# Adaptive-modulation sums in a two-layer trunk: the vector engine's multiply-add replaced by an activation-engine multiply and an accumulating DMA

## The chip, the cores and the metric

The kernel runs on one core of one Trainium2 chip. The metric is the device time of one execution in microseconds (us), as the median of several runs. The profile is one more execution of the same program, recorded instruction by instruction.

## The reference

Two layers of a trunk with 512 tokens of width 1024, all in float32. Each layer has two sub-layers (a token mixer, then a squared-ReLU MLP with 4096 hidden units); layer 0 mixes with chunked attention (16 heads of 64), layer 1 with a gated spatial MLP. Around every sub-layer stands a modulation that depends on the vector `c` alone:

```python
cond = jax.nn.silu(c)
for i in range(DEPTH):                                  # DEPTH = 2
    mod = cond @ ada_w[i] + ada_b[i]                    # (1, 1024) @ (1024, 6144)
    sh1, sc1, g1, sh2, sc2, g2 = jnp.split(mod, 6, axis=-1)
    h = rms_norm(x, norm_mix[i]) * (1.0 + sc1) + sh1
    y = mixer(h)                                        # attention, then gMLP
    x = x + g1 * y
    h = rms_norm(x, norm_ffn[i]) * (1.0 + sc2) + sh2
    x = x + g2 * squared_relu_mlp(h, ffn_w1[i], ffn_w2[i])
```

The change concerns `cond @ ada_w[i]`, a product of one row with a matrix. There are 12 such products of 1024 by 1024, called (layer, m) with m = 0 to 5 for `sh1, sc1, g1, sh2, sc2, g2`.

## The kernel before, in words

**Matrix products.** Nearly all time goes to TensorE. Each float32 operand is split into a high part (a cast on ACT) and a low part (a subtraction on DVE), and each product is three matmuls (`mm3`; line 92 is the one call to the matmul). Weights come by DMAs that SP issues; lines 388/389 (`wload`), 405/406 (`wload_slabs`) and 483/484 (`Split`) are the casts and subtractions.

**Buffers.** All large tiles are 4 KB per partition and come from 49 slots in a ring (`Slots`): `get` takes the slot longest free, `free` puts it at the end. A DMA into a slot waits until the last reader of its former content is done, and SP issues its DMAs in order, so one late release holds up all loads behind it.

**Order.** The program's text gives priorities, and a planner with a simulated timeline fixes, before the run, the order of the instructions on every engine. Stretches between `in_order` and `any_order` keep the text's order on the engines named (always on PE). `tc.issue_after(x)` keeps the instructions of its block, on x's engine alone, behind x. On the chip each engine then works off its own list in that order and stops at any instruction whose inputs are late.

**Modulation.** The first two vectors, (0, 0) and (0, 1), are made by special code in the opening 70 us (line 948) and are not touched. The other ten go through a background queue `bgq`, in the order (0,2), (0,4), (0,3), (0,5), (1,1), (1,0), (1,2), (1,4), (1,3), (1,5). Each of them is nine items: eight parts and one end.

- A part loads 128 partitions x 1024 columns of `ada_w` (512 KB, line 179, issued by SP) into a slot `raw`. Row p, part k holds weight row 8p + k. `use` multiplies it by `cs[:, k]`, one number for each partition, and adds it to `acc`: line 192 for part 0 (a multiply into `acc`), line 194 for parts 1 to 7. Then `done()` frees `raw`.
- The end adds up the 128 partitions of `acc`. For m = 0, 1, 3, 4 (`ada_columns`): eight transposes on PE (line 207), reductions on DVE (208), the bias and the gain. For m = 2, 5 (`ada_rows`): a cast on ACT (232), a subtraction on DVE (233), matmuls with a matrix of ones through line 92, and the bias added on DVE (240).

`bg(n)` takes n items off the queue at chosen places of the text: 27 items during attention (2 after the key projection, 5 around the first head, then 2 a head for eight heads and 1 a head for four), 27 in the first MLP and the first part of layer 1, three at a time in the MLP, and the rest in the gate, in the `u` blocks and in the second MLP. In attention an item is loaded as it is taken; from the first MLP on, `lead[0] = 2` loads two items ahead. The uses run inside `behind()`, which is `tc.issue_after(mark[0].ins)`; `mark` is always a DVE instruction.

**Attention.** For each head, `head_a` loads a bias tile and POOL (GpSimd) clears a corner of it (line 1168); for each second head it makes keys and queries (lines 1139 to 1153, with SBUF to SBUF copies that SP issues at 1153). `head_b` multiplies scores on PE, then takes bias and row maxima on DVE (1190) and the exponential on ACT (1195); POOL widens the reciprocals for each pair (1200). `head_c` transposes (1228) and splits (1232, 1233); `head_d` multiplies by the values and applies POOL's widened rows (1263, 1265). `filler` puts the remaining projections between the heads. Apart from a few fills at the start, POOL has no other work than lines 1168, 1200 and two fills at 1475.

Of the kernel before, what the change touches and what calls it, by code (L numbers as in the profile page):

```python
# [12 lines left out]
AF = mybir.ActivationFunctionType  # L13
ALU = mybir.AluOpType
# [38 lines left out]
def trunk_kernel(  # L53
# [20 lines left out]
    V, A, G, T, SP = nc.vector, nc.scalar, nc.gpsimd, nc.tensor, nc.sync  # L74
# [80 lines left out]
    def raw_tile(shape):  # L155

        t, i = SL.get(shape, F32)
        return t, lambda: SL.free(i)

    def flat(src, offset, ap):  # L160
        return bass.AP(tensor=src.tensor, offset=src.offset + offset, ap=ap)
# [6 lines left out]
    def ada_acc(l, ms, c0, n, box):  # L168


        nm = len(ms)
        kl = D // n // nm

        def load(k0):
            box[k0] = raw, done = raw_tile([P, kl, nm * n])
            if nm == 1:
                w, base = (4096, D * 2048 - 2048) if l == 0 else (6144, D * 6144)
                src = flat(ada_w, base + k0 * w + ms[0] * D, [[KD * w, P], [1, D]])
                SP.dma_start(raw[:, 0, :], src)
            else:  # L180
                src = flat(ada_w, (c0 // n * P * KD + k0) * 512, [[KD * 512, P], [1, kl * 512]])
                SP.dma_start(raw.rearrange("p k n -> p (k n)"), src)

        def use(k0):
            if k0 == 0:
                box["acc"], box["id"] = SL.get([P, nm * n], F32)
            acc = box["acc"]
            raw, done = box.pop(k0)
            for k in range(k0, k0 + kl):
                r, ck = raw[:, k - k0, :], cs[:, k:k + 1]  # L190
                if k == 0:
                    V.tensor_scalar(acc, r, ck, None, ALU.mult)
                else:
                    V.scalar_tensor_tensor(acc, r, ck, acc, ALU.mult, ALU.add)  # L194
            done()

        return [(lambda k=k: load(k), lambda k=k: use(k)) for k in range(0, KD, kl)]
# [324 lines left out]
    class Spent:  # L522
# [33 lines left out]
        def done(self, m):  # L556
            self.op.pop(m).free()
# [1080 lines left out]
```

## Time and profile before

| | |
|---|---|
| median of 3 runs | 1421.3 us (1420.83 to 1423.51) |
| the profiled execution | 1422.04 us |
| its span in the trace | 1420.1 us |
| matmuls on PE | 1390.1 us busy, 98% of the span |
| DVE / ACT / POOL | 1021.5 / 712.1 / 9.1 us busy |
| moved by DMAs | 208.94 MB |

How to read it: PE, DVE, ACT, POOL and SP are TensorE, VectorE, ScalarE, GpSimd and SyncE; PEld is the loading of TensorE's weights. L194 is line 194 of the kernel. "A <- B" in a group of instructions means that A writes and B is read (s a slot, p a PSUM bank); in a view of waits it means that A waited for B. A "q" behind an engine's name is its instruction queue, so SPq is SP issuing DMAs. "The chain that ended last" is followed back from the last instruction, at each step to what released it. PE's busy time comes from modelled ends, so a busy PE may still lose some of its pace; its granted clock (PEclk, 1.00 is full) stands in the views by stretches.

### The profile page before, as it was taken

What the parts mean: (1) busy time and instruction counts of PE and PEld (TensorE: products, weight loads), DVE (VectorE), ACT (ScalarE), POOL (GpSimd) and SP (SyncE); (2) the same over time, 40 slices, a digit from 0 to 9 for tenths busy, and PEclk for the clock granted to TensorE, in tenths of its full rate; (3) what the DMA queues carried; (4) which work ended last, traced back from release to release, by engine and by line L of the source; (5) the groups of instructions that cost most, each with busy time, mean ns of one, the idle gap of its engine ahead of it and who ended that gap; (6) DMA issues with size and microseconds to landing.
All of it is one profiled execution on the core that took longest, in us unless ns stands there. A gap on an engine that the chain in (4) does not pass through costs nothing.

```text
span 1420.1 us, 18904 instructions
## 1 busy us (share of the span) xinstructions
PE 1390.1 (98%) x7222; PEld 1191.5 (84%) x7222; DVE 1021.5 (72%) x1494; ACT 712.1 (50%) x1230; POOL 9.1 (1%) x34
## 2 busy tenths in 40 slices
PE   9999989899999999999999999999999999999998
PEld 8888888779888888888888887888889988888887
DVE  6888889585676887786895745657577376766883
ACT  6546658555464544447577343134346355454630
POOL 0000000000000000000000000000000000000000
PEclk8999999999999999999999999999999999999999
DMA  9656465574245361357133344335337225142041
GB/s 373 236 152 205 141 190 150 181 258 157 63 152 186 119 212 55 111 190 263 60 104 119 119 133 134 97 127 185 119 119 280 77 75 192 53 156 89 30 163 60
DMA packets 82171, 208.94 MB, mean 147 GB/s; under 512 B 7576, under 2 KB 8992, under 8 KB 82080
## 3 DMA queue, kind: packets, MB, share of 16 engines
q1 hardware_dynamic: 82080, 207.72, 44.6%
q8 instruction: 57, 0.93, 0.3%
q14 instruction: 34, 0.28, 0.1%
HBM read 190.92 MB, written 8.39 MB: 140 GB/s over the span
## 4 chain that ended last, share of the span: by engine, by line
PE 86%; DMA 6%; DVE 5%; ACT 1%; issue 1%; SPq 0%; DVEq 0%; ACTq 0%
PE p L92 84%; DMA s<-in_ada_w 2%; DMA s<-in_a_w_in 2%; DMA s<-in_ffn_w 1%; DMA s<-s 1%; PE p L1536 1%; DVE s L194 1%; DVE s L389 1%; DVE s L1190 1%; PE p L315 1%; DMA s<-in_b_w_in 0%; DMA s<-in_a_w_out 0%; PE p L1228 0%; DVE s L1144 0%; DVE s L948 0%
## 5 line engine op out<-in xcount | busy, mean ns | idle before, releaser
L92 PE MATMUL p<-s,s 128*128 128x512 f32 (+3 forms) x6568 | 1327.6, 362 | 11.5 <-DVE s L1233 4.3
L92 PEld LDWEIGHTS p<-s,s 128*128 128x128 f32 x6568 | 1114.3, 190 | 198.0 <-DVE s L1233 4.9
L484 DVE TENSOR_TENSOR s<-s,s 128x1024 fp32r<-128x1024 f32 x234 | 280.6, 1221 | 112.1 <-PE p L92 53.8
L483 ACT CAST s<-s 128x1024 fp32r<-128x1024 f32 x234 | 241.6, 1051 | 176.3 <-PE p L92 111.3
L389 DVE TENSOR_TENSOR s<-s,s 128x1024 fp32r<-128x1024 f32 x80 | 96.6, 1221 | 60.8 <-ACT s L388 54.2
L388 ACT CAST s<-s 128x1024 fp32r<-128x1024 f32 x80 | 83.7, 1052 | 81.7 <-DMA s<-in_b_w_in 28.1
L631 DVE TENSOR_TENSOR s<-s,s 128x1024 f32<-128x1024 f32 x64 | 77.4, 1221 | 37.0 <-DMA s<-in_ffn_w 33.9
L194 DVE SCALAR_TENSOR_TENSOR s<-s,cs,s 128x1024 f32<-128x1024 f32 x70 | 89.7, 1281 | 12.3 <-DMA s<-in_ada_w 11.4
L739 ACT ACTIVATE r<-p 128x512 f32<-128x512 f32 x64 | 38.1, 595 | 115.2 <-PE p L92 115.2
L517 DVE TENSOR_TENSOR s<-p,s 128x512 f32<-128x512 f32 x104 | 70.6, 687 | 34.5 <-PE p L92 33.3
L745 ACT ACTIVATE s<-r 128x256 f32<-128x256 f32 (+1 forms) x112 | 44.9, 443 | 1.2
L424 DVE TENSOR_TENSOR tr<-p,s 128x512 f32<-128x512 f32 (+1 forms) x33 | 22.0, 672 | 30.3 <-PE p L92 30.1
L1195 ACT ACTIVATE s<-s,nm 128x128 f32<-128x128 f32 (+3 forms) x64 | 35.7, 560 | 6.3 <-DVE nm L1190 6.2
L1517 ACT CAST s<-s 128x512 fp32r<-128x512 f32 x24 | 14.5, 620 | 44.1 <-DVE s L1515 25.6
L1228 PE MATMUL p<-ident,s 128*128 128x128 f32 x160 | 25.3, 277 | 11.1 <-DVE s L1265 2.7
L1542 DVE TENSOR_TENSOR s<-p,s 128x256 fp32r<-128x256 f32 x48 | 20.0, 419 | 21.7 <-ACT s L1541 21.7
L1513 ACT ACTIVATE s<-p 128x512 f32<-128x512 f32 x24 | 14.4, 598 | 39.9 <-PE p L92 39.7
L530 DVE TENSOR_TENSOR s<-s,s 128x1024 f32<-128x1024 f32 x28 | 33.6, 1220 | 1.0 <-PE p L92 0.9
L304 ACT ACTIVATE s<-s 128x512 f32<-128x512 f32 x24 | 15.3, 636 | 35.5 <-DVE s L425 35.5
L1190 DVE CUSTOM_DVE_ANT_0 s<-p,s 128x128 f32<-128x128 f32 (+3 forms) x64 | 29.1, 486 | 4.6 <-PE p L92 2.7
L1228 PEld LDWEIGHTS p<-ident,s 128*128 128x128 f32 x160 | 18.4, 141 | 14.7 <-ACT s L1305 3.0
L1233 DVE TENSOR_TENSOR s<-p,s 128x512 fp32r<-128x512 f32 (+3 forms) x64 | 28.9, 484 | 2.4 <-ACT s L1232 2.2
(142 smaller groups left out, 766.5 us busy)
## 6 DMA issues: line engine op xcount, KB each, us to landing
s<-in_ffn_w SPq DMA_DIRECT2D x128, 512.0 KB, 4.6
s<-in_ada_w SPq DMA_DIRECT2D x96, 512.0 KB, 4.7
s<-in_b_w_in SPq DMA_DIRECT2D x48, 512.0 KB, 4.7
s<-in_b_w_out SPq DMA_DIRECT2D x24, 512.0 KB, 4.6
s<-in_a_w_in SPq DMA_DIRECT2D x22, 512.0 KB, 5.0
s<-s SPq DMA_DIRECT2D x64, 128.0 KB, 2.6
s<-in_x SPq DMA_DIRECT2D x8, 512.0 KB, 5.0
s<-in_a_rel_bias SPq DMA_DIRECT2D x16, 256.0 KB, 2.9
```

What stands on the lines that cost most here:

```text
L92: T.matmul(ps, lhsT, rhs, start=start, stop=stop, skip_group_check=more)
L194: V.scalar_tensor_tensor(acc, r, ck, acc, ALU.mult, ALU.add)
L388: A.copy(hi, raw)
L389: engs[len(ids) // 2 % len(engs)].tensor_tensor(lo, raw, f32(hi), ALU.subtract)
L483: A.copy(self.hi, raw)
L484: mark[0] = V.tensor_tensor(self.lo, raw, f32(self.hi), ALU.subtract)
L517: V.tensor_tensor(dst, ps, dst, ALU.add)
L631: V.tensor_tensor(x[0], y_[0], z[0], ALU.subtract)
L739: A.activation(r, ps, AF.Relu)
L745: A.activation(d, v, AF.Square)
L1190: V.tensor_tensor_reduce(out=pt[it], in0=ps[:, 0:n], in1=b["bias"][:, 512 - n:512], scale=-1.0, scalar=-NEG, op0=ALU.add, op1=ALU.min, acc ...
L1228: T.transpose(ps[:, it * P:(it + 1) * P], b["pt"][it][:, jt * P:(jt + 1) * P], ident)
```

## The change

Part 0 of each of the ten sums moves from DVE to ACT. Parts 1 to 7 are multiplied on ACT in place, inside `raw`, and then added to `acc` by a DMA from SBUF to SBUF that POOL issues, with the addition done on the way. `raw` is freed after that DMA has read it. The loads, the ends, the places of `bg` and the opening (line 948) stay as they are.

```diff
             for k in range(k0, k0 + kl):
                 r, ck = raw[:, k - k0, :], cs[:, k:k + 1]
                 if k == 0:
-                    V.tensor_scalar(acc, r, ck, None, ALU.mult)
+                    A.activation(acc, r, AF.Copy, scale=ck)
                 else:
-                    V.scalar_tensor_tensor(acc, r, ck, acc, ALU.mult, ALU.add)
+                    A.activation(r, r, AF.Copy, scale=ck)
+                    G.dma_start(acc, r, accum_op=ALU.add)
             done()
```

## The prediction

> **What bounds the kernel now.** I read the busy times first, then the stretches, then the chain of waits through attention, then the parts themselves on DVE.
>
> ```profile
> PE   1390.1 (98%) x7222; PEld 1191.5 (84%) x7222; DVE 1021.5 (72%) x1494; ACT 712.1 (50%) x1230; POOL 9.1 (1%) x34
> 76.00:250.00 174.00, 159.82 (x1171) 149.60 (x1170) 150.72 (x366) 109.97 (x264) 6.43 (x22) 0.97 0.60 172
> 325.00:852.00 527.00, 527.00 (x2533) 444.43 (x2532) 389.87 (x432) 285.43 (x449) 0.61 (x2) 1.00 0.40 134
> 925.00:1420.00 495.00, 491.11 (x2436) 416.82 (x2433) 329.29 (x400) 214.38 (x324) 0.00 (x0) 1.00 0.37 123
> ```
>
> The first row is from the page; the others give, for a stretch, its length, the busy time of PE, PEld, DVE, ACT and POOL, the granted clock, the DMA engines' share and GB/s. The reader is to see two kernels in one. From 325 us on PE is busy all the time (527.00 of 527.00; the last stretch loses only its tail) at full clock: an easier DVE can win nothing there, and anything that makes PE wait is lost. In attention (76 to 250 us) PE idles 174 - 159.82 = 14.2 us, and a clock of 0.97 costs some 0.03 x 174 = 5.2 us more: 19.4 us is the most that a change can win. DVE is busy 150.72 of 174 us there (87%), so DVE is what relief would have to come from.
>
> ```profile
> by line: PE p L92 50.3%; DMA s<-s 3.4%; DMA s<-in_ada_w 3.4%; issue 3.3%; DVE s L194 3.2%; DMA s<-in_a_w_in 2.9%; DVE s L1190 2.9%; DMA s<-in_a_w_out 2.4%; PE p L1228 2.2%; DMA s<-in_ffn_w 2.2%; DVE s L1144 2.1%; DVE s L1233 2.0%; DVE s L40
> ```
>
> This is the chain from 70 to 325 us, by line. L194 is 3.2% of 255 us = 8.2 us of it. But DMAs that are waited for inside attention (s<-s, in_ada_w, in_a_w_in) make 9.7%, 24.7 us, three times as much.
>
> **The change, part by part.**
>
> *1. Off DVE.*
>
> ```profile
> L194 DVE SCALAR_TENSOR_TENSOR s<-s,cs,s 128x1024 f32<-128x1024 f32 x70 | 89.7, 1281 | 12.3 <-DMA s<-in_ada_w 11.4
> L192 DVE TENSOR_SCALAR s<-s,cs 128x1024 f32<-128x1024 f32 x10 | 7.5, 748 | 0.0
> 76.00:250.00 174.00, 26.88 (x21) 0.97 0.60 172
> ```
>
> The third row is L194 alone in the stretch: 21 of the 70 multiply-adds, 26.9 us. The other 49 lie under a saturated PE, cover that is there with or without them, and win nothing. Of the 26.9 us, 8.2 us stand on the chain; the rest runs while something else is last. I take **-8**; bounds 0 (DMA latencies come last in their place) and -19 (all of PE's loss).
>
> *2. Onto ACT.*
>
> ```profile
> L908 ACT ACTIVATE s<-s,ru 128x1024 f32<-128x1024 f32 x1 | 1.1, 1148 | 0.2 <-DVE ru L903 0.2
> DVE s L194 <- DMA s<-in_ada_w: 6.2, 3, 2.9
> ```
>
> L908 is the same instruction on the same shape: 1.15 us, 80 times, 92 us in all. Attention gets 24 of them, 28 us: ACT goes from 110 to 138 of 174 us, still the less busy of the two. The second row is from the waits of 76 to 250 us: the wait for late loads (3 times, 6.2 us) moves to ACT's list, ahead of the exponentials and casts that PE needs. `behind()` holds only DVE instructions, so ACT's part may also run earlier than DVE's did. I take **+2**; bounds 0 (ACT is free 37% of the stretch) and +7 (each multiply takes its L194's place on the chain, 8.2 x 1.15 / 1.28). Nothing is won or lost under MLP: ACT has 285 of 527 us there.
>
> *3. The accumulating DMA.* No row of before shows one. Nearest rows:
>
> ```profile
> s<-s SPq DMA_DIRECT2D x64, 128.0 KB, 2.6
> xs<-s SPq DMA_DIRECT2D x8, 512.0 KB, 3.1
> s<-in_ada_w SPq DMA_DIRECT2D x96, 512.0 KB, 4.7
> L1153 SPq DMA_DIRECT2D s<-s x64: 461/595/1394, 91.4 to 244.9; - x64
> ```
>
> (Issue to landing; the last row is the time that SP needs to issue one.) In attention the engines moved 172 GB/s at a share of 0.60, so 1 MB costs 3.5 us of all sixteen and 512 KB (0.524 MB) 1.83 us. The 128 KB copy has 0.46 us of that, which leaves 2.1 us fixed. An addition must read `raw` and `acc` and write `acc`; taken as two passes: 2.1 + 2 x 1.83 + 0.6 for issuing = **6.4 us**. Ends: 3.1 us (the store of the same bytes, nothing read back) and 2.1 + 4 x 1.83 + 0.6 = 10 us (adding at half the pace). I stay near the two-pass value, which lies by the 4.7 us row plus one more pass.
>
> [...]
>
> *4. The additions run one after the other.* Each reads and writes the same `acc`, so POOL, in order, holds each until the one before has landed.
>
> ```profile
> 70.75 0.74 DVE L192 TENSOR_SCALAR s<-s,cs 128x1024 f32<-128x1024 f32 x1
> 97.99 1.28 DVE L194 SCALAR_TENSOR_TENSOR s<-s,cs,s 128x1024 f32<-128x1024 f32 x1
> 217.46 1.28 DVE L194 SCALAR_TENSOR_TENSOR s<-s,cs,s 128x1024 f32<-128x1024 f32 x1
> 79.31 3.95 SPq L179 DMA_DIRECT2D s<-in_ada_w  x2
> 99.34 1.05 ACT L232 CAST s<-s 128x1024 fp32r<-128x1024 f32 x1 [2.06 <-DMA s<-in_a_rel_bias]
> 105.38 0.62 PE L92 MATMUL p<-s,ones 128*128 128x512 f32 x2
> 99.70 0.14 POOL L1168 MEMSET s<- 64x64 f32 x1 [12.19 <-DMA s<-in_a_rel_bias]
> 124.44 0.27 DVE L1190 CUSTOM_DVE_ANT_0 s<-p,s 128x128 f32<-128x128 f32 x1
> ```
>
> All loads of (0,2) are out by 83 us, so its seven additions are bound by their own chain: from 71.9 us (70.75 + 1.15) to 71.9 + 7 x 6.4 = 116.7 us, against 99.3 us (the second row's end). That is 17.4 us late, and the cast at 99.34 and the ones-matmuls at 105.38, which stood 6 us behind, go with it. PE's list is fixed, so the scores behind those matmuls wait, unless the planner knew how long an addition takes. Its miss on loads is 2 us each (6.2 over 3); with six links behind the first, 6 x 2 = 12 us. I take **+11**, between 0 (the planner is right, the matmuls stand later) and +17. It does not add up over the three sums: all 21 additions need 134 us, and 71.9 to 218.7 us, where DVE had them, is 146.8 us. On POOL's own list the additions are ahead of bias corners and widened rows: the corner cleared at 99.70 (head 3) is first read at 124.44, 24.7 us later, which covers 17 us of lateness, but not 35.
>
> *5. More traffic in attention.* 21 additions of 3.7 us (two passes) are 77 us of all sixteen engines on top of 0.60 x 174 = 104 us: the share would be 1.04, full; with one pass it is 0.82. The 24.7 us of DMA on the chain would stretch by a third: **+8**; bounds 0 (the traffic falls into gaps) and +25 (they double).
>
> *6. SP's list.* `raw` is given back when the addition has landed, so SP's waits that now end on L194 end some 5 us later:
>
> ```profile
> SPq L712 <- DVE s L194: 27.1, 5, 11.3
> SPq L625 <- DVE s L194: 12.2, 3, 8.5
> ```
>
> Those loads run three steps ahead of their matmuls, and PE waited for none of them: 0. Without that lead it would be 8 waits x 5 us = 40 us, which I keep for the upper end.
>
> *7. The ends behind attention.* Where loads are two items ahead, the additions can begin when a part lands, long before DVE's turn:
>
> ```profile
> 432.90 5.77 SPq L179 DMA_DIRECT2D s<-in_ada_w  x2
> 477.87 1.28 DVE L194 SCALAR_TENSOR_TENSOR s<-s,cs,s 128x1024 f32<-128x1024 f32 x1
> 486.84 1.29 DVE L208 TENSOR_REDUCE mod<-p 128x4 f32<-128x512 f32 x2 [0.26 <-PE p L207]
> 686.72 0.82 SPq L179 DMA_DIRECT2D s<-in_ada_w  x2
> 691.72 2.60 DVE L194 SCALAR_TENSOR_TENSOR s<-s,cs,s 128x1024 f32<-128x1024 f32 x2 [3.20 <-DMA s<-in_ada_w]
> 695.61 1.22 DVE L233 TENSOR_TENSOR s<-s,s 128x1024 fp32r<-128x1024 f32 x1
> ```
>
> For (1,1) the last loads land near 443; 1.15 + 2 x 6.4 later is 457, ahead of the reduction at 486.84. For (1,2) they land near 692, additions end at 706 and the subtraction of 695.61 comes 12 us later; its matmuls can hold PE so long. One exposed end of that kind, part of it foreseen by the planner: **+4**; bounds 0 and +24 (two such ends in full).
>
> **Sum.** -8 + 2 + 11 + 8 + 4 = +17 us on the profiled time of 1422.0 (span 1420.1, 1.9 around it): 1439. The median of the runs, 1421.3, is 0.7 lower: **1438 us**. The own range of this case, from its smaller ends (-15 + 1 + 8 + 5 + 2) and larger ones (-4 + 4 + 16 + 15 + 10): 1422 to 1462.
>
> **The rivals.**
>
> *A, faster: relief wins.* An addition takes 4 us or less. Then (0,2) is done by 71.9 + 28 = 100 us, as before, nothing is late on PE, and with one pass the traffic is hidden. For it: DVE at 87% and PE's losses in attention; against it: the 4.7 us of a plain load. It decides from (99.3 - 71.9) / 7 = 3.9 us down. Price: -8 to -15 + 2, so 1411 (1406 to 1418).
>
> *B, much slower: POOL paces attention.* From 146.8 / 21 = 7.0 us an addition up, the chain of additions is longer than the stretch that held them. At 9 us it is 189 us, 42 us too long; the corners and widened rows behind it outrun their 24.7 us cover. Sum: -8 + 2 + 42 (in place of 11) + 8 + 8 = +52, 1473 (1452 to 1500). For it: the engines' share; against it: nothing but my estimate of 6.4.
>
> *C, nothing to see.* Relief and lateness cancel, or the planner has placed every end late enough: -8 + 2 + 6 = 0, 1421 (1418.5 to 1424).
>
> **How the numbers follow.** Forecast 0.45, A 0.23, B 0.18, C 0.14. The range 1411 to 1475 leaves out about half of A and half of B, 0.2. Below 1418.5 or above 1424.1 (0.2%, about what a measurement can tell here) counts as a difference: faster 0.24, same 0.15, slower 0.61.
>
> **What would show it.** In the changed trace: DVE about 97 us less busy, ACT 92 us more; 70 issues on POOL, 6 to 7 us to landing (under 4: A; over 7: B); PE idle in 76 to 250 us above 14.2 us, waiting at the ones-matmuls of (0,2) or behind late bias corners; a DMA share there of 0.8 or more; 325 to 852 us no longer quite full. The prediction is wrong if the additions land in 4 us, if the planner's order puts the ends far behind them, or if the attention heads are reordered so that DVE's relief is worth its full 19 us.

## The result, and the profile after

The changed kernel takes 1470.3 us (median of 5 runs, 1462.6 to 1478.6) against 1421.3 (1418.4 to 1423.5) on the same chip: a ratio of 1.0334 with a 95% interval of 1.0303 to 1.0366. It is 49 us slower, where 17 were forecast. The profiled span is 1468.6 us, against 1420.1.

The page of the changed kernel: busy time, one DMA queue (its share is that of all sixteen engines), the groups of the new operations, and the DMA issues (KB each, us to landing). The last row is the source view of line 195, the new DMA. Lines behind 194 stand one higher than before.

```profile
PE 1409.4 (96%) x7222; PEld 1204.1 (82%) x7222; DVE 931.9 (63%) x1414; ACT 793.7 (54%) x1310; POOL 69.5 (5%) x104
q0 software_dynamic: 10080, 36.70, 13.3%
L194 ACT ACTIVATE s<-s,cs 128x1024 f32<-128x1024 f32 x70 | 80.6, 1153 | 87.8 <-DMA s<-in_ada_w 87.3
L195 POOL DMA_DIRECT2D s<-s x70 | 60.4, 862 | 965.7 <-ACT s L194 423.0
s<-s POOLq DMA_DIRECT2D x70, 512.0 KB, 6.2
DMA to landing us min/median/max: 4.5/6.2/10.0
```

The change does what it says: DVE is 89.6 us less busy, ACT 81.6 more, and 70 additions go out on POOL. In the median one lands 6.2 us after its issue. Their engine time is 0.133 x 1468.6 / 70 = 2.8 us of all sixteen each.

The views by stretches, in the columns of the prediction:

```profile
76.00:250.00 174.00, 144.18 (x975) 135.29 (x974) 105.77 (x283) 105.44 (x225) 21.16 (x36) 0.88 0.77 196
497.00:532.00 35.00, 31.19 (x130) 25.31 (x130) 28.16 (x33) 21.18 (x28) 0.86 (x1) 0.90 0.40 121
746.00:781.00 35.00, 31.21 (x128) 24.16 (x127) 33.46 (x33) 24.38 (x38) 0.00 (x0) 0.95 0.37 121
```

DVE is no longer the busy engine of attention (105.8 of 174 us, from 150.7), and yet PE idles 29.8 us there instead of 14.2, with the granted clock at 0.88 instead of 0.97. Both losses are of one size: 15.6 us more idling, and, by an estimate from the two clocks, about 0.09 x 174 = 15.7 us of pace. The same work side by side says it too: PE's first 1802 matmuls, done at 307.0 us before and at 337.4 after, take 283.28 us of busy time before, at a granted clock of 0.96, and 297.48 after, at 0.91, so of 30.4 us 14.2 are pace and 16.2 idling. Behind attention, where PE had been full, two holes stand at 497 and 746 us, and the clock is lower in them too (0.90 and 0.95, against 1.00 in 325 to 852 us before). What lowers it no view shows; in attention it is lower where PE is less busy (0.97 at 159.8 us busy of 174, 0.88 at 144.2).

Where the loss arises is read by laying the same pieces of PE's work side by side in the two chains that ended last (start, length). Before:

```profile
306.99 1.09 PE p L315 x8
628.89 10.90 PE p L92 x48
777.79 18.46 PE p L92 x85
1092.12 324.23 PE p L92 x1588
```

After:

```profile
337.36 1.09 PE p L316 x8
668.77 10.91 PE p L92 x48
824.10 18.46 PE p L92 x85
1140.34 324.23 PE p L92 x1588
```

At the transposes behind attention 30.4 us are lost; then 39.9, 46.3 and 48.2. So attention lost 30 us and the rest 18, nearly all before 824.

Pieces of the chain of the changed kernel at the start of attention, from 62.09 to 102.45 (short pieces between them left out), and at three places behind it:

```profile
62.09 9.78 DMA s<-s
...
72.17 4.56 DMA s<-s
...
77.01 4.52 DMA s<-s
...
82.06 4.51 DMA s<-s
86.64 0.33 SPq L1168
...
87.55 7.53 DMA s<-in_ada_w
95.10 1.16 ACT s L194
...
96.55 5.84 DMA s<-s
102.45 1.04 ACT s L406
...
476.82 8.70 DMA s<-s
486.05 6.33 DMA s<-s
492.67 4.55 DMA s<-s
498.19 2.00 ACT s L484 x2
583.46 9.81 DMA s<-s
593.32 1.10 PE p L208 x8
740.48 4.57 DMA s<-s
745.14 1.24 DVE s L485
```

This is the picture of the loss. Additions stand back to back, link behind link, and the chain leaves them by a different door each time (a door is the place where a late addition stops other work): at 86.64 into SP, which could not issue a bias load (1168) because its slot was still the source of an addition; from there to a late load of `ada_w`, another addition, and at 102.45 to a cast of the projection's weights (406), which has nothing to do with modulation; at 498 and 745 into the casts and subtractions of the MLP's weights, whose output slots were still being read; only at 593 into an end (PE's transposes, line 208).

The waits behind those doors: in the whole run, then in 60 to 330 us, then SP's queue in 60 to 330 us (total us, times, longest).

```profile
POOL s L195 <- DMA s<-s: 196.2, 36, 9.1
DVE s L485 <- DMA s<-s: 29.8, 6, 6.6
ACT s L484 <- DMA s<-s: 26.7, 8, 8.5
...
POOL s L195 <- ACT s L194: 43.3, 10, 8.2
POOL s L195 <- DMA s<-s: 33.2, 7, 9.1
...
SPq L1168 <- DMA s<-s: 32.5, 5, 24.5
SPq L401 <- DMA s<-s: 21.8, 4, 9.6
```

POOL waits 36 times for its own previous addition. In attention it waits longer for ACT's products (43.3 us) than for that, so it does not simply run at its limit there.

How the first door reaches PE can be followed further. The first two rows are from PE's list in order of time, the others are waits (60 to 330 us, then the whole run):

```profile
97.89 1.09 PE L1140 MATMUL p<-ident,s 128*128 128x128 f32 x4 [8.15 <-DVE s L1145]
118.60 0.62 PE L92 MATMUL p<-s,ones 128*128 128x512 f32 x2
ACT s L194 <- DMA s<-in_ada_w: 33.3, 10, 10.0
PE p L208 <- DMA s<-s: 3.2, 2, 1.9
```

SP stands still for 24.5 us until it can issue the bias load at 86.64, and issues the next load of `ada_w` behind it. ACT's multiply of that part, at 95.10, waits 10.0 us for the load, the making of keys and queries (1144, 1145) stands behind it on ACT's list, and PE stops 8.15 us for these. So PE comes to the ones-matmuls of (0,2) at 118.60 instead of 105.38, 13 us late, before any end has held it. For the accumulator of a late sum PE itself waits twice, 3.2 us in the whole run.

### The profile page after: what moved, and what is told of

The parts are those of the page before. It is cut to its first block, busy times and chain, and to the rows that moved or that the text cites. A ratio compares the mean times of both kernels' runs of the same rounds, so it can differ in the third digit from the quotient of the medians.

```text
span 1468.6 us, 19087 instructions
## 1 busy us (share of the span) xinstructions
PE 1409.4 (96%) x7222; PEld 1204.1 (82%) x7222; DVE 931.9 (63%) x1414; ACT 793.7 (54%) x1310; POOL 69.5 (5%) x104
## 3 DMA queue, kind: packets, MB, share of 16 engines
q0 software_dynamic: 10080, 36.70, 13.3%
## 4 chain that ended last, share of the span: by engine, by line
PE 70%; DMA 16%; ACT 5%; DVE 4%; issue 2%; SPq 1%; POOL 0%; ACTq 0%; DVEq 0%; POOLq 0%
PE p L92 68%; DMA s<-s 9%; DMA s<-in_ada_w 5%; ACT s L194 1%; DVE s L485 1%; DVE s L949 1%; ACT s L484 1%; DMA s<-in_ffn_w 1%; PE p L1537 1%; DMA s<-in_b_w_in 1%; SPq L1154 1%; DMA s<-in_b_w_out 0%; ACT s L406 0%; PE p L316 0%; DVE s L390 0%
## 5 line engine op out<-in xcount | busy, mean ns | idle before, releaser
L485 DVE TENSOR_TENSOR s<-s,s 128x1024 fp32r<-128x1024 f32 x234 | 279.6, 1219 | 172.4 <-ACT s L484 80.5
L390 DVE TENSOR_TENSOR s<-s,s 128x1024 fp32r<-128x1024 f32 x80 | 96.8, 1221 | 56.6 <-ACT s L389 51.5
L194 ACT ACTIVATE s<-s,cs 128x1024 f32<-128x1024 f32 x70 | 80.6, 1153 | 87.8 <-DMA s<-in_ada_w 87.3
L195 POOL DMA_DIRECT2D s<-s x70 | 60.4, 862 | 965.7 <-ACT s L194 423.0
L632 DVE TENSOR_TENSOR s<-s,s 128x1024 f32<-128x1024 f32 x64 | 77.3, 1219 | 34.7 <-DMA s<-in_ffn_w 34.3
L1532 DVE SCALAR_TENSOR_TENSOR s<-p,bsT,s 128x384 f32<-128x384 f32 (+2 forms) x48 | 20.8, 477 | 23.8 <-PE p L92 19.6
L531 DVE TENSOR_TENSOR s<-s,s 128x1024 f32<-128x1024 f32 x28 | 33.5, 1217 | 0.1
L407 DVE TENSOR_TENSOR s<-s,s 128x1024 fp32r<-128x1024 f32 x18 | 21.4, 1220 | 16.6 <-DMA s<-s 8.5
## 6 DMA issues: line engine op xcount, KB each, us to landing
s<-s SPq DMA_DIRECT2D x64, 128.0 KB, 3.3
```

The lines of the kernel that those rows point to most:

```text
L194: A.activation(r, r, AF.Copy, scale=ck)
L195: G.dma_start(acc, r, accum_op=ALU.add)
L390: engs[len(ids) // 2 % len(engs)].tensor_tensor(lo, raw, f32(hi), ALU.subtract)
L485: mark[0] = V.tensor_tensor(self.lo, raw, f32(self.hi), ALU.subtract)
L632: V.tensor_tensor(x[0], y_[0], z[0], ALU.subtract)
```

## The experiments

Each is the kernel before with the body of `use` changed, unless said; the diffs are shortened to the lines that matter, and some remarks behind a # are added here. The planner orders each one anew (PE's list stays in the text's order), so a few microseconds can come from another order on the other engines; no run holds that order fixed. Times are compared with the kernel before on the same chip. "Lateness" is how much later than before POOL's eighth widened row starts, near the end of attention; the changed kernel has 32.2 us.

**The multiply alone.** The addition stays on DVE.

```diff
-                    V.scalar_tensor_tensor(acc, r, ck, acc, ALU.mult, ALU.add)
+                    A.activation(r, r, AF.Copy, scale=ck)
+                    V.tensor_tensor(acc, acc, r, ALU.add)
```

(Part 0 on ACT as in the change.)

> ACT multiplies every part in place as in the changed kernel, but DVE adds it to acc; no DMA adds anything. Three theories for the 49 us. (L) Lateness: the additions by DMA follow one another at about 6.2 us, sums end late, and PE's fixed list stops at the ends. (S) Slots: raw stays taken until its addition has landed, and SP, which issues in order, and the engines that write into the recycled slot are held. (A) ACT: its list now stops at multiplies that wait for loads (87.3 us in 42 waits in the changed kernel, against 11.4 us in 6 on DVE before), with exponentials and casts behind. Here only (A) is left, with DVE as loaded as before: (A) expects +20 us or more over before, 1441 or more; (L) and (S) expect 1415 to 1428.

Measured: 1413.9 us, 0.9927 (0.9901 to 0.9952). It is faster than both kernels. Its stretch:

```profile
76.00:250.00 174.00, 163.93 (x1202) 152.89 (x1201) 158.04 (x383) 133.31 (x298) 9.35 (x22) 0.98 0.62 183
```

ACT at 133 us of 174 harms nothing, so ACT's multiplies alone are not the cause; in the changed kernel they pass the delay on because their loads are late (10.0 us at 95.10). PE is 4 us busier there than before. DVE's addition (1.22 us) is hardly shorter than the multiply-add (1.28), so why all 10 us were won is not settled; that ACT's multiply is not tied to `behind()` and takes a part as soon as it lands was only argued.

**The DMA alone.** DVE multiplies.

```diff
-                    V.scalar_tensor_tensor(acc, r, ck, acc, ALU.mult, ALU.add)
+                    V.tensor_scalar(r, r, ck, None, ALU.mult)
+                    G.dma_start(acc, r, accum_op=ALU.add)
```

> DVE multiplies every part in place (0.75 us instead of 1.28), POOL's DMA adds it as in the changed kernel; ACT has nothing new. (L) and (S) expect most of the loss, +35 to +50 us over before, 1456 to 1471. (A) expects less than +15 us, under 1436.

Measured: 1495.3 us, 1.0496 (1.0474 to 1.0517). The whole loss, and more, comes with the accumulating DMA; moving the multiply softens it.

**By place.** The change for (0,2), (0,4), (0,3) alone, and for the other seven sums alone.

```diff
+                moved = (l, ms[0]) in ((0, 2), (0, 4), (0, 3))    # and "not in"
```

> The change for the three sums made during attention only, (0,2), (0,4), (0,3): 21 additions by DMA; the other seven sums as before. The two traces set against each other put 30 us of the loss before the first norm transposes of the MLP and 18 us behind: all theories expect +27 to +33 us, 1448 to 1454, if the two places do not depend on each other; my prediction's terms had +13 here.

> The change for the seven later sums only: 49 additions by DMA, with loads two items ahead. From the two traces: +18 us, 1436 to 1443. My prediction's term was +4 (1425); if the later loss is only a consequence of the first stage being late, 1421 to 1426.

Measured: 1453.9 us, 1.0203 (1.0182 to 1.0224), and 1442.1, 1.0121 (1.0095 to 1.0146): +30 and +18, as the milestones of the two chains say, and together the whole.

**Traffic and the holding of a slot.** Both stand on the first experiment, whose sums are never late. One adds a plain store of each product by POOL into one DRAM buffer (so the stores run one after the other, POOL waiting 29 times and 128.0 us for the one before, and hold `raw`), the other a copy of 512 KB from DRAM to DRAM for each part, into four buffers in turn, which holds no slot (POOL's short read before it holds `raw` a little longer).

```diff
+                    G.dma_start(side[0, :, :], r)                    # the store
+                    tick = G.tensor_copy(tock, r[:, 0:1])            # the copy
+                    with tc.issue_after(tick.ins):
+                        G.dma_start(side[k % 4, :, :], x[0, 0:P, :])
```

> The fast form of before (ACT multiplies, DVE adds: 1414 us) with one plain store of each multiplied part into a scratch array in memory, issued by POOL, one after the other. No sum waits for it: lateness is out. (S) slots: raw stays taken until the store has landed, 3 to 4 us a store against 6.2 us an addition; expects +15 to +35 over 1414, 1429 to 1449. (T) traffic: one pass of 512 KB for 70 parts, a bit more than half of an addition; expects +10 to +25, 1424 to 1439. (L) lateness of the sums expects no loss, 1411 to 1418.

> The same fast form with traffic alone: after each addition by DVE, POOL reads one column of the multiplied part (a short instruction that gives the time) and then issues a 512 KB copy from memory to memory that touches no slot and that nobody waits for. (T) expects +10 us or more over 1414, 1424 to 1450. (S) and (L) expect 1411 to 1419.

Measured: 1415.4 us, 0.9938 (0.9918 to 0.9959), and 1424.4, 1.0004 (0.9988 to 1.0021). The store's page and stretch:

```profile
side<-s POOLq DMA_DIRECT2D x70, 512.0 KB, 4.3
76.00:250.00 174.00, 163.39 (x1196) 151.60 (x1195) 158.48 (x382) 130.82 (x292) 16.32 (x40) 0.99 0.75 237
```

The store moves the same 36.70 MB at nearly the changed kernel's share in attention (0.75 against 0.77), and no loss shows: this traffic is hidden, and so is a slot held 4.3 us. It is no full stand-in for the additions, as its queue took 6.6% of the engines' span and theirs 13.3%. The copy, which also reads DRAM and has POOL read each part first, cost some 10 us over the first experiment, 4 of them by POOL's eighth widened row (262.07 us against 257.62); the 10 are the low end of what (T) had expected. So traffic is not excluded as a part of the loss.

**Half the chain.** In attention each sum gets two accumulators, for odd and even parts, which DVE adds up at the end.

```diff
+                elif moved and k == 1:
+                    box["odd"], box["oid"] = SL.get([P, nm * n], F32)
+                    A.activation(box["odd"], r, AF.Copy, scale=ck)
                 elif moved:
                     A.activation(r, r, AF.Copy, scale=ck)
-                    G.dma_start(acc, r, accum_op=ALU.add)
+                    G.dma_start(box["odd"] if k % 2 else acc, r, accum_op=ALU.add)
+                if moved and k == KD - 1:
+                    V.tensor_tensor(acc, acc, box["odd"], ALU.add)
```

> The change in the three sums of attention only (1454 us with one chain), with two accumulators, one for even and one for odd parts, so that the chain of additions is half as long; DVE adds the two at the end; 6 of 7 additions by DMA stay. (L) expects most of the 30 us to go: 1424 to 1436. (T) expects nearly the whole loss to stay, 1447 to 1455. (S) expects a part: a raw part no longer waits behind its predecessor, but holds its own 6.2 us: 1434 to 1448.

Measured: 1429.1 us, 1.0039 (1.0016 to 1.0062), against 1.0203 with one accumulator. Of the 30 us of the change in attention some 23 are gone, though an addition still takes some 6 us (6.20 and 6.05 in the chain that ended last) and 18 of the 21 stay. Its stretch, and the wait of POOL for its own additions in 60 to 330 us:

```profile
76.00:250.00 174.00, 159.79 (x1158) 149.03 (x1158) 131.24 (x346) 123.33 (x271) 18.70 (x35) 0.96 0.80 211
POOL s L202 <- DMA s<-s: 5.5, 1, 5.5
```

The DMA share is even higher (0.80); PE and the clock are back where they were, and PE's stop of 8 us for keys and queries is gone. In attention it is in the main the length of the chain, not its bytes.

**Which door.** On the change in attention alone: slots given back four parts later in the background queue (so that SP asks for one later), ends queued three parts later, and both.

```diff
-            done()
+            held.append(done)                      # slots four parts later
+            for _ in range(len(held) - (0 if k0 == KD - 1 and ms[0] == 3 else 4)):
+                held.pop(0)()
...
-        bgq.extend(ada_mod(l, m))
+        items = ada_mod(l, m)                      # ends three parts later
+        bgq.extend(items[:3])
+        bgq.extend(owed)
+        owed = [items[8]] if (l, m) in ((0, 2), (0, 4)) else []
+        bgq.extend(items[3:8] if owed else items[3:])
```

> The change in the three sums of attention only (1454 us), with the slot of each part given back to the ring four parts later, so that whoever takes it next comes after the addition has landed; chain and traffic are unchanged. (S) expects most of the 30 us to go: 1424 to 1438. (L) and (T) expect 1448 to 1458.

> The change in the three sums of attention only (1454 us), with the ends of (0,2) and (0,4) taken from the queue three parts of the next sum later, so that their accumulators have been complete for some time; (0,3) keeps its place. Chain, traffic and slots as there. If late ends are the exit by which the chain costs time: 1430 to 1440. If slots are the exit: 1449 to 1457. If each takes over from the other (giving slots back late alone brought 5 us): 1443 to 1452.

> Both exits closed for the sums of attention: ends of (0,2) and (0,4) later, and each part's slot given back four parts later. If ends and slots together are how the chain costs time: 1424 to 1436, as with two accumulators (1429). If something else about the additions counts (their traffic, their place on POOL's list, ACT waiting for loads): 1443 to 1455.

Measured: 1.0181 (1.0151 to 1.0211), 1.0162 (1.0136 to 1.0188), 1.0137 (1.0107 to 1.0166), against 1.0203 (1.0182 to 1.0224): by these ratios 3, 6 and 9 us fewer than the 30. The first two intervals overlap that of the change in attention alone, so only the gain of both edits together is clear of the noise. With slots late, the ends hold PE longer (8.4 us in 60 to 330 us, 2.2 without that edit):

```profile
PE p L221 <- DMA s<-s: 8.4, 2, 8.2
```

and with both, SP still waits for slots (its queue, 60 to 330 us):

```profile
SPq L1186 <- DMA s<-s: 36.7, 5, 12.9
```

PE's longest stop for keys and queries, 7.9 us in the change for attention alone, is still 7.9, 8.7 and 6.7 us in the three runs, and 0.4 us with two accumulators; so these edits leave the slot door largely open, and what it is worth by itself is not measured by them.

**Each door by itself, without the other.** On the first experiment: six small serial DMAs on 16 columns of `acc` at the end of each sum (late ends; hardly a byte, no slot but that of `acc`), and two serial stores for each part (slots and POOL behind a long chain; no sum waits for a store).

```diff
+                if k == KD - 1:                                      # late ends
+                    for _ in range(3):
+                        G.dma_start(side[0, :, 0:16], acc[:, 0:16])
+                        G.dma_start(acc[:, 0:16], side[0, :, 0:16])
...
+                    G.dma_start(side[0, :, :], r)                    # held slots
+                    G.dma_start(side[0, :, :], r)
```

> The fast form (1414 us), in which only the end of each sum is made late: after the last part, six small DMAs one after the other write 64 bytes a partition of acc out and back in, some 13 us in all, with nearly no bytes and no slot held but acc itself. (L) expects the loss of late ends, +8 us or more for the ten sums over 1414: 1422 to 1445. (S) and POOL's list expect 1411 to 1419. If the planner places the ends' work as late as the DMAs really take, 1411 to 1417, and lateness costs only where the real time is above the planned one.

> The fast form (ACT multiplies, DVE adds, 1414 us), with two stores of each part by POOL into the same scratch array, one after the other (one store each cost nothing: 1415 us, chain step 3.2 to 4 us). The chain on POOL is now 6 to 9 us a part, at least as long as with additions, raw is held to its end and POOL is held too, but no sum waits for it. (S) slots behind a chain of this length expects +20 to +50 over 1414: 1434 to 1464. (L) the lateness of the sums themselves expects 1411 to 1420. POOL's own late work (bias corners, widened rows) would also show here, as 1425 or more.

Measured: 1439.8 us, 1.0102 (1.0065 to 1.014), and 1464.6, 1.0274 (1.0233 to 1.0315): 26 and 51 us over the first experiment, of which 18 and 43 in attention (lateness) and some 8 to 12 each behind it. Stretches:

```profile
76.00:250.00 174.00, 156.56 (x1125) 145.70 (x1124) 145.91 (x351) 120.21 (x264) 15.60 (x38) 0.94 0.55 161
```

```profile
76.00:250.00 174.00, 142.18 (x965) 131.21 (x964) 128.64 (x307) 106.67 (x228) 23.49 (x52) 0.89 0.74 247
side<-s POOLq DMA_DIRECT2D x140, 512.0 KB, 3.8
```

With late ends PE is less busy and the clock lower (156.6 us and 0.94, against 163.9 and 0.98), though these DMAs stand on POOL's list too. Slots held by a long chain alone do so as far as the change did (142.2 us and 0.89 against 144.2 and 0.88), with no sum behind the stores. The second is no clean separation: 42 stores x 3.8 = 160 us are more than the 146.8 us that the sums had, so POOL's pace is in it.

**POOL's other work.** The change in attention alone, with bias corners and widened rows moved to DVE.

```diff
-        G.memset(b["bias"][0:64, 448:512], NEG)
+        V.memset(b["bias"][0:64, 448:512], NEG)
...
-            G.tensor_copy(
+            V.tensor_copy(
```

> The change in the three sums of attention only (1454 us), with the bias corners and the widened reciprocals moved from POOL to DVE, so that nothing but additions stands on POOL's list. If heads wait for POOL's list behind additions (rival B of the prediction): 1425 to 1440. (L) and (S): 1447 to 1458.

Measured: 1452.4 us, 1.0194 (1.0154 to 1.0234), against 1.0203. Nothing is won: the work that stands behind the additions on POOL's list is not where the loss goes.

**Another adder.** ACT multiplies, POOL adds by an instruction of its own.

```diff
-                    G.dma_start(acc, r, accum_op=ALU.add)
+                    G.tensor_tensor(acc, acc, r, ALU.add)
```

> ACT multiplies, POOL itself adds (a two-input add of 128x1024), no DMA and nothing on DVE: the relief that the change was about, without its chain. If an add on POOL takes 3 us or less and does not hold DVE, attention gains what DVE loses: 1400 to 1414. If POOL's adds hold up DVE or are as slow as a DMA: 1420 to 1445.

Measured: 1433.9 us, 1.0075 (1.0049 to 1.0101): a link of 2.6 us instead of 6.2, and +10 instead of +49. Its groups:

```profile
L195 POOL TENSOR_TENSOR s<-s,s 128x1024 f32<-128x1024 f32 x70 | 181.1, 2588 | 826.5 <-ACT s L194 512.4 <-ACT s L192 303.2 <-ACT s L1233 4.1
L485 DVE TENSOR_TENSOR s<-s,s 128x1024 fp32r<-128x1024 f32 x234 | 308.3, 1341 | 129.4 <-ACT s L484 70.8 <-PE p L92 53.0 <-issue 3.3
```

DVE's subtractions of the weights, 1219 ns in the changed kernel, take 1341 here, 10% more on the mean. Other groups of DVE are longer too: L632 takes 1285 ns against 1219, L307 (one tile read) 1087 against 754, L326 (a cast) 512 against 291; L531 does not (1218 against 1217). That POOL's additions held them was not followed from instruction to instruction. So this +10 us need not be the price of the chain alone.

**Half the chain behind attention.** All sums changed, two accumulators in eight of the ten; (1,1) and (1,0) keep one, for want of a free slot.

```diff
-                moved = (l, ms[0]) in ((0, 2), (0, 4), (0, 3))
+                moved, pair = True, (l, ms[0]) not in ((1, 1), (1, 0))
```

> The change in all ten sums (1470 us), with two accumulators in eight of them; (1,1) and (1,0) keep one chain, since no slot is free for a second accumulator there. In attention alone two accumulators took 25 us away. If the chain's length also makes the loss behind attention: 1470 - 25 - 9 or so, 1431 to 1440. If that loss has another cause: 1442 to 1449.

Measured: 1459.0 us, 1.0237 (1.0199 to 1.0274), some 13 us less loss than the changed kernel. Attention's lateness falls from 32 to 10 us, but behind attention some 26 us are lost instead of 18. The miss matters: halving the chain does not help there, and DVE's subtractions still wait up to 11.2 us for slots. The second accumulator takes one more slot in stretches where few are free; that this is the reason was not shown.

## Why the prediction was right or wrong

*Direction and picture.* Slower was right, and 1470 lies inside the range, near its upper end; the range reached so far for the sake of rival B, whose mechanism the runs do not bear out, so that is luck. The forecast of +17 was a third of the +49 measured: attention lost 30 us where terms 1 to 6 gave 13, and the rest lost 18 where term 7 gave 4.

*Terms 1 and 2 (relief, -8 + 2): not shown.* The multiply alone won 10 us, but without relief: DVE is as busy in attention as before (158.0 against 150.7 us, with more of the work done), so that the numbers lie close is no proof of term 1. The run that did relieve DVE without a DMA, with POOL adding, lost 10 us. In the changed kernel a gain, if there is one, is buried by the chain.

*Term 3 (an addition, 6.4 us): right.* 6.2 us, and even the plain store of the same bytes took 4.3.

*Term 4 (the serial chain, +11): this step failed, in its path.* That the additions run one behind the other was right, but their whole price was put on one door, PE's wait at the late end of (0,2). In the changed kernel PE waits 1.3 us for the cast and subtraction of such ends in the whole run, and 3.2 us for accumulators; it comes to the ones-matmuls of (0,2) 13 us late because of what it lost before them. That 13 lies near 11 is chance. Late ends can cost time (18 us in attention in the run that had only those), but here other work was late first.

*Term 6 (SP's list, 0): this step failed, and the first 13 us of attention went through it.* It argued that loads run three steps ahead. In the trace SP's bias load waited 24.5 us for a slot that an addition was reading, and from there the delay went on to a load of `ada_w`, ACT's multiply, the keys and queries and PE's stop of 8.15 us; SP's waits for DMAs from SBUF to SBUF come to some 62 us between 60 and 330 us, against 5 before. That slot was given back not 5 us late but a whole queue of additions late, since a part waited for all those ahead of it. The 40 us kept for the upper end was the right order. How the 30 us divide is not settled beyond the first 13, which arise before any end: the edits on slots or ends took 3 and 6 us, and both took 9; halving the chain, which shortens both, took 23.

*The clock was not in the sum as a loss.* It was read as 5.2 us to be won, not as something that could fall further: 14.2 of the 30.4 us that attention lost are pace (0.91 against 0.96 over the same 1802 matmuls).

*Term 5 (traffic, +8): its sizes were too large, its price is open.* An addition took 2.8 us of the engines, not 3.7, and the share came to 0.77 and not 1.04. Loads did land later (`ada_w` 5.8 us in the median, 4.7 before), but with the stores they also did (5.3), and no time was lost; the copy did cost 4 us in attention.

*Term 7 (ends behind attention, +4): too small, and only one of its doors.* The trace names one late end (593) and, at two other places (498 and 745), casts and subtractions that wait for slots; DVE and ACT wait 56.5 us for slots behind attention in all, while PE waits 1.9 us at that end. Two runs that had only late ends, or mainly held slots, lost some 8 to 12 us each there, which could make up the 18; that they add up was not tried, and the run with two accumulators speaks against chain length alone. So the division there stays open.

*Rival B* gave the right time (1452 to 1500) by a mechanism that the runs do not bear out: an addition takes 6.2 us and not 7, POOL waits longer for ACT than for itself in attention, and freeing POOL's list changed nothing. *Rival A* would have needed links under 3.9 us. *Rival C* is excluded by the interval.

## What to carry to other kernels

The DMAs that accumulated into one tile were a serial chain here (POOL waited 36 times, 196.2 us, for its own previous one): price such a chain by landing time times links, and ask not only who reads the sum, but who wants the buffers that each link still reads; here a load waited up to 24.5 us for one, a cast 8.5 and a subtraction 6.6. If it must be a chain, try a second accumulator where a buffer is free: it took 23 of 30 us in attention, and nothing behind it. Here the good half of the change was the cheap one: multiply on ACT, keep the add on DVE, 0.7% faster than before.

## What the runs showed of the hardware

- An accumulating DMA of 512 KB from SBUF to SBUF took 6.2 us to land (4.5 to 10.0), a plain store of the same size by POOL 3.8 to 4.3 in the median; issuing an addition kept POOL 0.86 us.
- Where POOL added, its addition of two 128x1024 tiles took 2.59 us, more than twice the 1.22 of DVE's in the first experiment, and DVE's subtractions of the weights took 1.34 us on the mean, 10% above the 1.22 of the changed kernel.
- In attention less work of PE mostly came with a lower clock: granted clock 0.98 at 163.9 us of PE work in 174, 0.96 at 159.8, 0.94 at 156.6, 0.88 at 144.2. They do not go in step: the run with slots given back later has 0.93 at 140.4.
